# Attention scores on one core: stores that read each partition's part of a tile as one run and write it as two

## The chip, the core and the metric

The kernel runs on one core of a Trainium2 chip. The metric is the device time of one execution in microseconds (us). A core has five engines that the profile names: PE (matrix products; its weight loads are shown apart as PEld), DVE (vector), ACT (scalar), POOL and SP. SP does no arithmetic here: it waits for semaphores and issues transfers. Transfers between the chip's memory (HBM) and the core's on-chip memory (SBUF, 128 partitions) are carried by 16 DMA engines, which the trace records packet by packet.

## What is computed

Scores of attention for 8 batches of 8 heads, each 512 rows of 64 numbers:

```python
def setup_inputs():
    batch, heads, seq, dim = 8, 8, 512, 64
    ...
def reference(q, k):
    scale = 1.0 / np.sqrt(q.shape[-1])
    return (np.einsum('bhqd,bhkd->bhqk', q, k) * scale).astype(np.float32)
```

Inputs are 16.78 MB, the output (8, 8, 512, 512) in float32 is 67.11 MB. All of both must pass the DMA engines once.

## The kernel before

**Tiles.** The output is made in 16 tiles of 4 MB, numbered `g`. Tile `g` belongs to batch `2 * (g // 4) + g % 2`. In one tile a partition holds 8 consecutive rows (`i`, `RO = 8`) of one head, and it does so for two heads (`x` = 0, 1). Eight rows of 512 float32 are 16 KB, so a partition's part of a tile is two blocks of 16 KB, 32 KB in all. In SBUF these two blocks lie one after the other: `big` has, for each partition, the shape (4 buffers, 2, 8, 512), and `bigs[g % 4]` is the buffer of tile `g`. In the output array the two blocks lie 4 MB apart (4 heads further on), and the blocks of neighbouring partitions lie side by side.

**Loads.** The four 2 MB slices of keys and of queries are loaded into the same buffers `big`. The first slice of keys is loaded in two halves of 1 MB, in pieces of 4 KB, one issued by SP and one by ACT (L72). The other seven (L83) are issued by SP one after the other, with runs of 16 KB on both sides.

**Compute.** POOL casts the loaded data to bf16 (`xb`, L126). DVE transposes keys into `kT` (L194) and queries into `qz` (L199). PE multiplies (L152): for each tile 16 products, in four groups of four, each group filling half of PSUM (the accumulation memory). ACT, or DVE for six of the groups, scales a group of four and writes it to `big` (L173, L171). Semaphores named `low*`, `high*`, `pe` and `out` order these; `free0` and `free1` count when a pair of buffers has been stored and may be overwritten.

**Stores.** SP's queue runs, after the loads, a loop over the tiles. Tile 0 is stored by itself as soon as `pe` shows that its last group has been taken, tile 1 by itself when `out` shows that it is complete (both L95, 4 MB each). From then on tiles 2 and 3, 4 and 5, and so on are stored in pairs, seven times 8 MB (L98), each when `out` counts the pair as complete. A pair occupies buffers 0 and 1 or buffers 2 and 3, so there are two pairs of buffers: while one pair is being stored, compute fills the other. When a store has landed it adds to `free0` or `free1`, and PE waits for that before it begins the next pair of tiles in these buffers.

The order of the work on each queue is written out by hand; there is no scheduler. Everything that the change touches is SP's store loop, lines 85 to 102 of the kernel before: the two calls of `dma_start` at L95 and L98. Each takes the tile as 128 partitions by 2 (or 4) pieces of 4096 numbers (16 KB) and the output in the same shape, where piece `b x` of the output is block `x` of batch `b`.

Of the kernel before, what the change touches and what calls it, by code (L numbers as in the profile page):

```python
# [5 lines left out]
def kernel(  # L6
# [5 lines left out]
    nc = tc.nc  # L12
# [4 lines left out]
    UNITS = B // 2  # L17
# [33 lines left out]
    big = nc.alloc_sbuf_tensor("big", [P, UNITS, 2, RO, S], f32)[:]  # L51
    bigs = [big[:, n] for n in range(UNITS)]
# [10 lines left out]
    def xf(v):  # L63
        return bigs[v].rearrange("p x i k -> p (x i k)").rearrange("p (x s c) -> p x s c", x=2, s=2)

    def slot(v, x):
        return v % SLOTS * 2 + x
# [3 lines left out]
    for s, queue in enumerate((nc.sync, nc.scalar)):  # L71
        first_load = queue.dma_start(  # L72
            out=xf(0)[:, 0, s].rearrange("p (x c) -> p x c", x=2), in_=k_0[s]
# [7 lines left out]
    for n in range(1, 2 * UNITS):  # L81
        v, x = divmod(n, 2)
        nc.sync.dma_start(out=xf(v)[:, x].rearrange("p s c -> p (s c)"), in_=(k_r, q_r)[x][v]  # L83
                          ).then_inc(load_sems[n], 16)
    for g in range(ALL):
        if g % 2:
            nc.sync.wait_ge(sem["out"], g // 2 + 1)
        elif g == 0:
            nc.sync.wait_ge(sem["pe"], 4 * g + 6)
        else:  # L90
            continue
        dst = out_r[g // 4, g // 2 % 2]
        free = sem[f"free{g // 2 % 2}"]
        if g < 2:
            nc.sync.dma_start(out=dst[:, g % 2 * 2:g % 2 * 2 + 2],  # L95
                              in_=bigs[g].rearrange("p x i k -> p x (i k)")).then_inc(free, 16)
        else:
            nc.sync.dma_start(out=dst, in_=big[:, g % UNITS - 1:g % UNITS + 1].rearrange(  # L98
                "p n x i k -> p (n x) (i k)")).then_inc(free, 32)
        if g % 2 and g < ALL - 1:  # L100
            nc.sync.sem_inc(sem[f"free{1 - g // 2 % 2}"], 1)  # L101
    for n in range(2):
# [4 lines left out]
    for v in range(UNITS):  # L107
# [3 lines left out]
        for x in range(2):  # L111
            if v or x:
                nc.gpsimd.wait_ge(load_sems[2 * v + x], 16)
            for s in range(2):
# [3 lines left out]
                dst = xb[:, slot(v, x)]  # L118
                if x == 0:
                    src = src.rearrange("p (w e d) -> p w e d", e=2, d=D)  # L120
                    dst = dst[:, s * J // 2:(s + 1) * J // 2].rearrange("p w d e -> p w e d")
                else:
                    src = src.rearrange("p (jj e i d) -> p jj e i d", e=2, i=RO, d=D)
                    dst = dst.rearrange("p (i jj) d e -> p jj e i d", i=RO)[
                        :, s * JJ // 2:(s + 1) * JJ // 2]
# [9 lines left out]
    with pe.Fori(0, ALL // 4):  # L135
        for t in range(4):
# [10 lines left out]
            for x in range(2):  # L147
                for i in range(RO):
                    if (x, i) in waits:
                        name, count = waits[x, i]  # L150
                        pe.wait_ge(sem[name], count)
                    ins = pe.matmul(out=ps[:, i], lhsT=qz[:, 2 * t + x, i], rhs=kT[:, 2 * t + x],  # L152
                                    start=True, stop=True)
                    if i % W == W - 1:
                        ins.then_inc(sem["pe"], 1)
                    elif (x, i) in takes:
                        name, count = takes[x, i]
# [105 lines left out]
```

## Time and profile before

| What | Value |
|---|---|
| time, median of 4 runs | 200.41 us (200.35 to 200.59) |
| time of the profiled execution | 200.4 us |
| its span, first to last instruction | 199.1 us |
| busy: PE / DVE / ACT / POOL | 82.3 / 113.9 / 105.9 / 38.9 us |
| moved by DMA | 83.90 MB: 16.78 read from HBM, 67.11 written |
| mean rate over the span | 421 GB/s |
| stores issued (SP's queue) | 2 of 4096 KB, 7 of 8192 KB |
| start of the stores' issue, us | 36.15, 42.13, 58.23, 78.28, 98.02, 117.15, 136.70, 156.29, 176.10 |
| time to issue a store / a load of L83 | 0.38 to 0.44 / 0.58 to 0.62 us |

The span is what the profiler saw between the first and the last instruction; the 1.3 us between it and the execution's time lie around it. The busy times of the engines add up to more than the span because they work side by side. A transfer is issued at one time and moves its bytes later: it stands behind earlier transfers of the same queue.

### The profile page before, as it was taken

The page shows a single profiled execution, that of the slowest core. Times are in us where ns is not written, and L with a number is a line of the kernel's source. Part 1 is how long each engine was busy: PE and PEld are TensorE (multiplying, and loading weights), DVE is VectorE, ACT ScalarE, POOL GpSimd, SP SyncE. Part 2 cuts the span into 40 slices and gives each one's busy share as a digit, 9 for nine tenths or more (in the row PEclk, how much of TensorE's full clock was granted, in tenths as well). Part 3 has the DMA queues.
Part 4 walks back from the last instruction along what each step waited for, and adds up shares of the span by engine and source line. Part 5 has one row for each costly group of instructions (what it writes and reads, how often), then busy time and mean ns, then how long its engine had stood idle before and what let it go on. Part 6 is the DMA issues. An engine that isn't in the chain of part 4 may idle for free.

```text
span 199.1 us, 725 instructions
## 1 busy us (share of the span) xinstructions
PE 82.3 (41%) x252; PEld 23.9 (12%) x256; DVE 113.9 (57%) x61; ACT 105.9 (53%) x59; POOL 38.9 (20%) x20
## 2 busy tenths in 40 slices
PE   0000357647524762576266516650776077600000
PEld 0000011111101110111021102110221021100000
DVE  4238999999477039943994599369926500400000
ACT  2000049969960977197629752974397349730000
POOL 0389999699000000000000000000000000000000
PEclk9999999988975799669859985999589658975555
DMA  6999999999999999999999999999999999999997
GB/s 182 444 428 425 435 428 431 428 418 431 428 431 438 425 438 428 431 435 425 435 428 438 431 426 435 423 438 435 428 435 425 435 438 425 435 425 428 425 431 316
DMA packets 5794, 83.90 MB, mean 421 GB/s; under 512 B 288, under 2 KB 288, under 8 KB 800
## 3 DMA queue, kind: packets, MB, share of 16 engines
q1 hardware_dynamic: 5520, 82.84, 97.8%
q10 hardware_dynamic: 272, 1.05, 1.3%
q14 instruction: 2, 0.02, 0.0%
HBM read 16.78 MB, written 67.11 MB: 421 GB/s over the span
## 4 chain that ended last, share of the span: by engine, by line
DMA 41%; ACT 30%; PE 9%; DVE 4%; POOL 2%; issue 1%; SPq 0%
DMA out_dram<-big 35%; ACT big L173 30%; PE ps L152 9%; DMA big<-in_q_dram 6%; DVE qz L199 4%; POOL xb L126 2%; SPq L95 0%; SPq L101 0%
## 5 line engine op out<-in xcount | busy, mean ns | idle before, releaser
L173 ACT ACTIVATE big<-ps 128x2048 f32<-128x2048 f32 x58 | 104.6, 1884 | 68.2 <-PE ps L152 68.2
L152 PE MATMUL ps<-kT,qz 128*128 128x512 bf16 x252 | 82.3, 465 | 91.7 <-DMA out_dram<-big 35.8
L199 DVE STREAM_TRANSPOSE qz<-xb 32x1024 f32<-32x1024 f32 (+1 forms) x36 | 65.2, 1810 | 1.5 <-POOL xb L126 0.9
L152 PEld LDWEIGHTS ps<-kT,qz 128*128 128x128 bf16 x256 | 23.9, 111 | 149.7 <-ACT big L173 47.9
L126 POOL CAST xb<-big 128x2048 bf16<-128x2048 f32 x16 | 38.7, 2468 | 10.4 <-DMA big<-in_k_dram 7.7
L171 DVE TENSOR_SCALAR big<-ps 128x2048 f32<-128x2048 f32 x6 | 13.8, 2292 | 43.8 <-PE ps L152 43.8
L194 DVE STREAM_TRANSPOSE kT<-xb 64x1024 f32<-64x1024 f32 (+1 forms) x18 | 31.5, 1749 | 10.9 <-POOL xb L126 6.7
L206 DVE MEMSET qz<- 128x4096 uint32 x1 | 3.5, 3472 | 2.9 <-PEq L77 2.9
L173 ACT ACT_TABLE_LOAD x1 | 1.3, 1283 | 2.0 <-PEq L77 2.0
L247 POOL MEMSET const-float32-0.0<- 128x1 f32 x1 | 0.1, 99 | 0.2 <-issue 0.2
L247 POOL MEMSET const-bfloat16-1.0<- 128x1 bf16 x1 | 0.1, 102 | 0.0
L247 POOL MEMSET const-uint8-127<- 128x1 uint8 x1 | 0.1, 102 | 0.0
L247 POOL MEMSET const-float32-1.0<- 128x1 f32 x1 | 0.1, 99 | 0.0
## 6 DMA issues: line engine op xcount, KB each, us to landing
out_dram<-big SPq DMA_DIRECT2D x7, 8192.0 KB
big<-in_q_dram SPq DMA_DIRECT2D x4, 2048.0 KB, 24.2
out_dram<-big SPq DMA_DIRECT2D x2, 4096.0 KB
big<-in_k_dram SPq DMA_DIRECT2D x3, 2048.0 KB, 24.2
big<-in_k_dram SPq DMA_DIRECT2D x1, 1024.0 KB, 7.4
big<-in_k_dram ACTq DMA_DIRECT2D x1, 1024.0 KB, 9.7
```

The costliest lines, as they stand in the source:

```text
L126: cast = nc.gpsimd.tensor_copy(out=dst, in_=src)
L152: ins = pe.matmul(out=ps[:, i], lhsT=qz[:, 2 * t + x, i], rhs=kT[:, 2 * t + x], start=True, stop=True)
L171: freed = nc.vector.tensor_scalar_mul(out=to, in0=src, scalar1=scale)
L173: freed = nc.scalar.mul(out=to, in_=src, mul=scale)
L194: return nc.vector.transpose(out=out, in_=src)
L199: return nc.vector.transpose(out=qw[d:d + Q, b % 2 * G:(b % 2 + 1) * G, rows, h * Q:(h + 1) * Q].rearrange("d g i (m jj) -> d i jj m g", j ...
L206: nc.vector.memset(qz, 0.0).then_inc(sem["zeroed"], 1)
L247: nc = _bacc.Bacc("TRN2", target_bir_lowering=False, num_devices=1)
```

## The change

The stores are no longer issued by `dma_start`, which gives both sides of a transfer the same shape. A new helper `store` builds the copy instruction itself. It takes the tile in SBUF as 128 partitions by 1 (or 2) runs of 8192 numbers (32 KB), and the output as 128 partitions by 2 (or 4) runs of 4096 numbers (16 KB) as before. Bytes, their order, addresses, the queue, the waits before the stores and the semaphores after them are the same. Loads and all work on the other engines are as before. The instruction is also no longer marked as precomputed by the building library, as `dma_start` marked the stores of before (the loads have no such mark in either kernel).

```diff
+    def store(to, tiles):
+        run = tiles.rearrange("p n x i k -> p n (x i k)")
+        return nc.sync.add_instruction(mybir.InstDMACopy(
+            name=nc.get_next_instruction_name(), engine=mybir.EngineType.SP, mode="Copy",
+            queue="qSPDynamicHW", ins=nc.sync.lower_ap_dma(run), outs=nc.sync.lower_ap_dma(to)))
+
     for g in range(ALL):
         if g % 2:
             nc.sync.wait_ge(sem["out"], g // 2 + 1)
...
         if g < 2:
-            nc.sync.dma_start(out=dst[:, g % 2 * 2:g % 2 * 2 + 2],
-                              in_=bigs[g].rearrange("p x i k -> p x (i k)")).then_inc(free, 16)
-        else:
-            nc.sync.dma_start(out=dst, in_=big[:, g % UNITS - 1:g % UNITS + 1].rearrange(
-                "p n x i k -> p (n x) (i k)")).then_inc(free, 32)
+            store(dst[:, g * 2:g * 2 + 2], big[:, g:g + 1]).then_inc(free, 16)
+        else:
+            store(dst, big[:, g % UNITS - 1:g % UNITS + 1]).then_inc(free, 32)
         if g % 2 and g < ALL - 1:
             nc.sync.sem_inc(sem[f"free{1 - g // 2 % 2}"], 1)
```

## The prediction, made before the changed kernel ran

> **What bounds the kernel now.** I read first the row of slices and the queue table of the page, to see whether any engine or the transfers fill the span. The DMA row is a busy share in tenths over 40 slices, the GB/s row is what the 16 DMA engines moved, and the queue rows give packets, MB and share of 16 engines' span.
>
> ```profile
> DMA  6999999999999999999999999999999999999997
> GB/s 182 444 428 425 435 428 431 428 418 431 428 431 438 425 438 428 431 435 425 435 428 438 431 426 435 423 438 435 428 435 425 435 438 425 435 425 428 425 431 316
> DMA packets 5794, 83.90 MB, mean 421 GB/s; under 512 B 288, under 2 KB 288, under 8 KB 800
> q1 hardware_dynamic: 5520, 82.84, 97.8%
> ```
>
> The transfers fill the span from the second slice to the last, at a rate that hardly moves; only start-up and the last landing are left out. The busiest compute engine, DVE, is at 57%. So any time must come out of the bytes' own rate, or out of a hole that the change would tear into it.
>
> Next the chain of waits (start us, length us, what), to see whether compute ever holds the transfers up.
>
> ```profile
> 58.23 23.75 DMA out_dram<-big
> 81.98 0.05 issue
> 82.03 1.90 PE ps L152 x4
> ...
> 94.35 3.65 ACT big L173 x2
> 98.01 0.02 issue
> 98.02 22.95 DMA out_dram<-big
> ```
>
> The chain puts 30% on ACT, which misleads alone: its steps run while the store of the other pair of tiles moves. The windows view settles it, in stretches of one 8 MB store each (stretch; its length; busy time by engine; granted clock, DMA share, GB/s).
>
> ```profile
> 61.40:80.83 19.43, 10.15 (x32) 2.96 (x32) 10.12 (x6) 12.60 (x7) 0.00 (x0) 0.85 1.01 432
> 80.83:100.26 19.43, 10.49 (x31) 3.00 (x32) 13.78 (x8) 12.71 (x7) 0.00 (x0) 0.76 1.01 432
> 119.70:139.13 19.43, 9.90 (x31) 2.92 (x32) 13.98 (x8) 12.60 (x7) 0.00 (x0) 0.85 1.01 431
> ```
>
> Each stretch is as long as the last, with a DMA share just over 1: the packets' recorded times overlap a little, and no compute wait opens a hole.
>
> **What one packet costs.** 67.11 MB written in pieces of 16 KB (16,384 bytes) are 4096 packets, 256 on each of 16 engines. This checks with the q1 row: 4096 of stores, 7 loads of 2 MB in 16 KB (896), 256 of the first key load's half in 4 KB, and 16 small ones for each of 17 transfers (272) make 5520. To split a packet's time into a part for bytes and a part for being a packet, I take the transfers in two windows: 62 to 176 us, stores alone, and 4 to 7 us, where only 4 KB packets run.
>
> ```profile
> DMA packets 3086, 49.20 MB, mean 432 GB/s; under 512 B 82, under 2 KB 82, under 8 KB 82
> q1 hardware_dynamic: 3084, 49.19, 100.7%
> ```
>
> ```profile
> DMA packets 309, 1.27 MB, mean 422 GB/s; under 512 B 0, under 2 KB 0, under 8 KB 309
> q1 hardware_dynamic: 155, 0.63, 51.9%
> q10 hardware_dynamic: 154, 0.63, 51.1%
> ```
>
> In the first, 3084 less 82 small ones are 3002 data packets: 16 x 114,000 ns / 3002 = 607.6 ns from one to the next on an engine, and 100.7% of that, 611.8 ns, is what one is recorded to take. So consecutive packets overlap by 4.2 ns. In the second, 16 x 3000 / 309 = 155.3 ns from one to the next, recorded at 103.0% of it, 160.0 ns. Four small packets carry the bytes of one large one, with three more packets: (4 x 155.3 - 607.6) / 3 = 4.5 ns for being a packet (one packet more or less in the 309 moves this by 0.7), which leaves 603.1 ns for 16 KB themselves. From recorded times, as if nothing overlapped, it is (640.0 - 611.8) / 3 = 9.4 ns.
>
> The small packets are loads and the large ones stores; that the fixed part is alike in both is my assumption.
>
> **The change, part by part.** (1) *Read runs.* Each tile's 32 KB in a partition is now one read run instead of two. That removes 128 read runs on each engine, 2048 in all. If the 4.5 ns belong to the read run, or to a packet that begins and ends with it, the gain is 128 x 4.5 = 0.58 us, all of it on the path that sets the end, since the engines are never idle in the store stage. Bounds: nothing gained, if the cost goes with a written piece; at most 128 x 9.4 = 1.20 us, if the saved packet start costs all that is recorded. I take 0.58, because spacing, not recorded length, is what fills a saturated stage.
>
> (2) *Write runs.* Their number, size, order and addresses stay: 256 on each engine, 16 KB each. What is new is that one read run feeds two of them. The trace of before has no such transfer. From below it costs nothing, or repays what (1) has; from above, the overlap between the pieces is lost (256 x 4.2 = 1.08 us). Farthest out, both written pieces and the read each pay 9.4 ns one after another: 128 x (3 x 9.4 - 2 x 4.5) = 2.46 us. I take nothing: the nearest row, 603.1 ns of bytes in 607.6, says that an engine streams one run into the next with almost no seam, and a seam inside one run should be no worse than that.
>
> (3) *Issue on SP.* The store's instruction is made by hand, with different shapes on its two sides. In the SP queue's rows (start us, us, engine, line) a store of before takes 0.40 us to issue and a load, whose two sides also differ in shape, 0.58.
>
> ```profile
> 2.65 0.58 SPq L83 DMA_DIRECT2D big<-in_k_dram  x1
> 78.28 0.40 SPq L98 DMA_DIRECT2D out_dram<-big  x1
> 98.02 0.39 SPq L98 DMA_DIRECT2D out_dram<-big  x1
> ```
>
> At worst that is 0.2 us more for each of 9 stores. Its cover is the store before: the one issued at 58.23 lands at 81.98, and the next is issued at 78.28, 3.70 us earlier. The first issue of the program, at 0.73, has moved no byte by 1.8 us in the trace, so about 1.1 us are start-up; allow another 1 us (an estimate from the last stretch, where the rate has fallen to 316 GB/s) between last byte and landing, and some 1.6 us are spare. So I cost it at nothing; were the cover gone, it would be 9 x 0.2 = 1.8 us. What is late next would be PE, which waits for the landing that frees a pair of tiles. No wait is added, and on PE, DVE, ACT and POOL nothing changes.
>
> Sum, against the profiled execution's own 200.4 us (span 199.1 and 1.3 around it): 200.4 - 0.58 + 0 + 0 = 199.8. The median of the runs is 200.41, so it holds there as well.
>
> The Trainium skill, page "DMA: Bandwidth & Descriptors", section "Why small descriptors are slow (HBM only)", names a fixed cost of about 3 cycles for a packet on trn2 beside 32 bytes a cycle; at the 850 MHz that the page gives for the fabric this is 3.5 ns and an estimate of 128 x 3.5 = 0.45 us, hence 199.95. The same section speaks against this change: it calls joining descriptors "only worth it at ≤256 B desc size", by which the sum would be nothing at 16 KB, 200.4. The windows above put a price on the packet at 16 KB, so here the size of the run does not make it free, only small.
>
> **The rivals.** *No change (200.4).* The 4.5 ns go with the written piece, of which there are as many as before, or the read run is cut again at 16 KB on its way, so that the change does not do what it says. For it: a record of before counts one packet per 16 KB and cannot tell which side it belongs to. Against it: only that reads and writes have the same number there, so nothing excludes it. The gain also falls into this case when a saved packet is worth under 0.40 / 128 = 3.1 ns; my 4.5 is not far above.
>
> *Slower (201.5).* At the seam inside the 32 KB run the second write cannot begin in the shadow of the first one's end, as separate packets do now: the 4.2 ns of overlap go at every piece, 1.08 us and 200.4 + 1.08 = 201.5, up to 202.9 by the far bound. It decides from 3.1 ns lost net in each 32 KB. For it: the overlap in the trace is one between packets, and the new packets are half as many; the stage has no idle time to hide any of it. Against it: bytes stream at 603.1 of 607.6 ns, which leaves little to lose. The late issue of (3) belongs to the slower side too, but needs 1.6 us to start.
>
> **How the numbers follow.** About 0.2%, 0.40 us, is what a measurement of this kernel can tell from no change. Forecast of a saved read run, 199.8, own range 199.2 to 200.0: 0.53. No change, 200.0 to 200.8: 0.23. Slower, at 201.5 for the most part: 0.24, of which 0.02 is the late issue. The likeliest gives the time, 199.8. The range starts at the largest gain, 200.4 - 1.20 = 199.2, takes in no change and reaches to the slower rival's 201.5; about 0.1 lies above, where the far bound is or the seam costs what no row shows, and 0.03 below.
>
> **What would show it.** Right: the stretch of one 8 MB store shrinks from 19.43 us to 19.43 - 16 x 0.0045 = 19.36 us, with the store window at about 433 to 434 GB/s, and the loads' part unchanged. If records follow read runs, q1 falls from 5520 to 3472 packets with a mean near 1215 ns; if they follow writes, the count stays and tells nothing. No change: stretches stay at 19.43. Slower: they grow to 19.5 or more with the DMA share still near 1 (a seam), or with slices under 9 between stores (late issue). I am wrong if the stretches stay while the total moves, or if a store's rate changes by over 1% either way, which no price above allows.

## The result and the profile after

The changed kernel takes 200.13 us (median of 40 runs, 199.96 to 200.30) against 200.41 us (60 runs, 200.29 to 200.62): 0.28 us less, a ratio of 0.9986 with a 95% interval of 0.9981 to 0.9990. The sign is the one forecast and the time lies in the range, but the gain is half of the 0.58 us predicted. It is under the 0.2% that the prediction took as the least that can be told from no change; the interval, a gain of 0.20 to 0.38 us, does tell it. The profiled execution took 200.05 us, with a span of 198.7.

The same rows of the page as before, now of the changed kernel:

```profile
GB/s 198 435 439 435 432 422 429 429 455 442 422 422 422 422 422 442 455 449 435 429 429 422 422 424 422 450 442 442 442 429 422 422 429 422 422 455 455 442 429 231
DMA packets 3746, 83.90 MB, mean 422 GB/s; under 512 B 288, under 2 KB 288, under 8 KB 800
q1 hardware_dynamic: 3472, 82.84, 97.2%
```

The trace counts read runs: q1 falls from 5520 packets to 3472, by exactly the 2048 reads removed. The change does what it says. (The rate of a slice now swings between 422 and 455 because a packet is entered whole where it starts, and a slice holds only four or so of them per engine.)

The stretches of one 8 MB store each, in the windows view of the changed kernel (stretch; length; busy time by engine; granted clock, DMA share, GB/s). Every engine closes a store with a packet of 4 bytes; the bounds, here and before, are where the first of the 16 engines does so.

```profile
61.28:80.65 19.37, 9.81 (x32) 2.89 (x32) 10.72 (x6) 12.60 (x7) 0.00 (x0) 0.85 1.00 433
80.65:100.02 19.37, 10.21 (x31) 3.01 (x32) 14.05 (x8) 12.60 (x7) 0.00 (x0) 0.76 1.00 433
119.39:138.76 19.37, 9.62 (x31) 2.89 (x32) 14.21 (x8) 12.60 (x7) 0.00 (x0) 0.85 1.01 433
177.51:196.88 19.37, 0.00 (x0) 0.00 (x0) 0.00 (x0) 0.00 (x0) 0.00 (x0) 0.50 1.00 433
```

19.37 us in place of 19.43, where 19.36 was predicted. So the DMA engine that leads saves nearly all that was forecast, and yet the end moves by half of it. The end is set by the engine that comes last. Its lag shows when the closing packets are counted in the transfers of two windows, the row's "under 512 B". Before:

```profile
DMA packets 14, 0.03 MB, mean 66 GB/s; under 512 B 12, under 2 KB 12, under 8 KB 12
...
DMA packets 4, 0.00 MB, mean 0 GB/s; under 512 B 4, under 2 KB 4, under 8 KB 4
```

That is 197.7 to 198.2 us, and 198.2 to 198.7: 12 engines close the last store in the first half microsecond, 4 in the next. After, in 196.8 to 197.5 and 197.5 to 198.3:

```profile
DMA packets 15, 0.03 MB, mean 47 GB/s; under 512 B 14, under 2 KB 14, under 8 KB 14
...
DMA packets 2, 0.00 MB, mean 0 GB/s; under 512 B 2, under 2 KB 2, under 8 KB 2
```

Fourteen engines are done by 197.5, earlier than the first one before (197.71), and two stragglers set the end, the last at 198.23 where the last before was 198.60. From the first engine to the last it was 0.89 us before and is 1.34 us after. (These are two single executions, 200.40 and 200.05 us; by the medians the gain is 0.28.) That is the place where expected gain went missing; the experiments ask what a read run is worth, and what the stragglers owe their lag to.

### The profile page after: what moved, and what is told of

The parts are those of the page before. It is cut to its first block, busy times and chain, and to the rows that moved or that the text cites. A ratio compares the mean times of both kernels' runs of the same rounds, so it can differ in the third digit from the quotient of the medians.

```text
span 198.7 us, 725 instructions
## 1 busy us (share of the span) xinstructions
PE 81.2 (41%) x252; PEld 23.7 (12%) x256; DVE 113.9 (57%) x61; ACT 105.7 (53%) x59; POOL 38.9 (20%) x20
## 3 DMA queue, kind: packets, MB, share of 16 engines
q1 hardware_dynamic: 3472, 82.84, 97.2%
## 4 chain that ended last, share of the span: by engine, by line
DMA 41%; ACT 33%; PE 6%; DVE 4%; POOL 2%; issue 0%; SPq 0%
DMA out_dram<-big 35%; ACT big L179 33%; PE ps L158 6%; DMA big<-in_q_dram 6%; DVE qz L205 4%; POOL xb L132 2%; SPq L89 0%; SPq L107 0%
## 5 line engine op out<-in xcount | busy, mean ns | idle before, releaser
L158 PE MATMUL ps<-kT,qz 128*128 128x512 bf16 x252 | 81.2, 459 | 92.3 <-DMA out_dram<-big 35.4
L212 DVE MEMSET qz<- 128x4096 uint32 x1 | 3.5, 3472 | 2.9 <-PEq L77 2.9
```

The lines of the kernel that those rows point to most:

```text
L212: nc.vector.memset(qz, 0.0).then_inc(sem["zeroed"], 1)
```

## The experiments

Three groups of runs: the cost of each side's runs, transfers without compute, and the same with a hole ahead of the stores.

### What belongs to the instruction, and what to the run

**equal16_byhand.** The changed kernel's helper, with 16 KB runs on the read side.

```diff
-        run = tiles.rearrange("p n x i k -> p n (x i k)")
+        run = tiles.rearrange("p n x i k -> p (n x) (i k)")
```

> The helper of the changed kernel, but with 16 KB runs on both sides, as the kernel before has them: only the way in which the instruction is made, and with it its issue on SP, differs from before. Theory (the gain is the saved read run or packet start): no gain is left, 200.41 us within 0.1, with 5520 packets on q1 in records of about 611 ns, and issues of about 0.61 us, as in the changed kernel, hidden behind the store before. Rival (the gain comes from the hand-made instruction): 200.13.

Measured 200.42 us against 200.40 of the kernel before beside it, ratio 1.0001 (0.9992 to 1.0010). On the page and in SP's queue (start us, us, engine, line):

```profile
q1 hardware_dynamic: 5520, 82.84, 97.7%
```

```profile
77.98 0.64 SPq L89 DMA_DIRECT2D out_dram<-big  x1
```

The issue is as long as in the changed kernel (0.64 us at 77.86 there, 0.40 before), and costs nothing that can be measured. The gain comes from the joined read runs and not from the way in which the instruction is made.

**flat_r32_w16, flat_r32_w32, flat_r32_w8.** The output's rows land in other places here, so that a partition's bytes are one stretch in HBM, and read and written runs can be chosen one by one (32 KB reads with 16, 32 or 8 KB writes). This is the edit for 16 KB writes; `e` in the first pair of lines is the read run in numbers of 4 bytes, in the second the written piece:

```diff
+    flat = out.rearrange("b h q k -> (b h q k)")
...
-        run = tiles.rearrange("p n x i k -> p n (x i k)")
+        run = tiles.rearrange("p n x i k -> p (n x i k)").rearrange("p (c e) -> p c e", e=8192)
...
-            store(dst, big[:, g % UNITS - 1:g % UNITS + 1]).then_inc(free, 32)
+            store(flat[(g - 1) * 2 ** 20:(g + 1) * 2 ** 20].rearrange("(p c e) -> p c e", p=P, e=4096), big[:, g % UNITS - 1:g % UNITS + 1]).then_inc(free, 32)
```

> The changed kernel with other addresses in the output: each partition's part of a tile or pair goes to one contiguous stretch of the output (rows land in other places), in the same 16 KB writes, fed by the same 32 KB reads. It is the base for the runs with other sizes. Both theories: 200.13 us if the distance between the two written blocks costs nothing. If far-apart blocks cost something, it is faster than that.

> As the base with contiguous output, but written in 32 KB runs as well: read and written runs are equal in number again, at half the number of before. Theory (a read run or packet start costs, a further written piece is free): the same as the base, within 0.1 us. Rival (a written piece costs as much as the read run, and a joined read saves only half of what a joined pair would): 128 x 3.5 ns = 0.45 us faster than the base, 199.7.

> As the base with contiguous output and 32 KB reads, but written in 8 KB pieces: 256 more written pieces on each engine. Theory (written pieces inside one read run are free): the same as the base, within 0.1 us. Rival (a written piece costs about 3.5 ns): 0.9 us slower than the base, 201.0.

Measured in this order, each against 200.40: 200.05 us (ratio 0.9982, 0.9973 to 0.9991), 200.11 (0.9985, 0.9976 to 0.9994) and 200.31 (0.9993, 0.9984 to 1.0002). Joining the written runs as well brings no time, against the rival that a written piece costs as much as a read run. But 8 KB pieces cost something, against the expectation that they are free. The stretches tell it apart, here two with 32 KB writes and then one with 8 KB:

```profile
61.23:80.59 19.36, 10.10 (x32) 2.97 (x32) 10.10 (x6) 12.60 (x7) 0.00 (x0) 0.85 1.00 433
80.59:99.95 19.36, 10.55 (x32) 3.02 (x32) 13.79 (x8) 12.71 (x7) 0.00 (x0) 0.76 1.01 435
```

```profile
61.45:80.90 19.45, 10.26 (x32) 3.02 (x32) 10.50 (x7) 12.60 (x7) 0.00 (x0) 0.76 1.00 431
```

**flat_r16_w8, flat_r8_w8.** The other way: two 8 KB pieces written for each 16 KB read, and 8 KB on both sides, by the sizes `e` of the same two lines.

> Full kernel, contiguous output, 16 KB reads as before, each written as two 8 KB pieces. Theory (the read run costs, a second written piece within it about 1 ns): 256 x 1.2 = 0.3 us slower than the kernel before at most, 200.4 to 200.7. Rival (a written piece costs like a read run): 201.6, like the run with 8 KB on both sides.

> Full kernel, contiguous output, 8 KB runs on both sides: 256 more read runs and 256 more written pieces on each engine than with 16 KB on both (512 each). Theory (about 4.6 ns for each packet that begins with a read run): 256 x 4.6 = 1.2 us slower than the kernel before, 201.6, with records near 309 ns. If the end follows an engine that is late for other reasons, less than that.

Measured 200.56 us against 200.40 (1.0012, 1.0003 to 1.0020), as expected: written pieces are not priced like read runs. (Its stretch 61.46 to 80.93 takes 19.47 us, which is 0.04 / 32 = 1.3 ns for each added seam between two written pieces.) With 8 KB on both sides 202.85 us (1.0122, 1.0108 to 1.0137), twice the expected loss. Its stretches show two regimes:

```profile
61.63:81.21 19.58, 10.54 (x32) 3.02 (x32) 10.44 (x6) 12.71 (x7) 0.00 (x0) 0.76 1.01 428
...
120.65:140.68 20.03, 9.88 (x32) 2.91 (x32) 13.91 (x8) 12.60 (x7) 0.00 (x0) 0.84 1.01 419
```

At first a store takes 0.15 us more than before for 32 more read runs on each engine, (19.58 - 19.43) / 32 = 4.7 ns each, as predicted (4.6). From about 100 us on it takes 20.0. Something else sets in. By size, (20.03 - 19.58) / 64 = 7.0 ns for each read run, it is what the runs with a hole show further below; but in the trace from 130 to 132 us the starts of the packets do not gather as they do there, so its cause stays open.

From these stretches, taken over four stores (77.73 us before, 77.48 in the changed kernel, 77.43 with 32 KB writes): a saved read run is worth (77.73 - 77.43) / 64 = 4.7 ns, and the seam between two written pieces costs (77.48 - 77.43) / 64 = 0.8 ns, which leaves 3.9 ns for each join in the changed kernel, 0.50 us over its 128. (The bounds are read to 0.01 us, which moves each of these prices by some 0.2 ns.)

### Transfers alone, with and without a hole

All work on PE, DVE, ACT and POOL is left out in the next four runs; the loaded data is stored in place of scores, in the same nine stores.

**bare_r16_w16, bare_r32_w16.** The stores begin when all loads have landed.

```diff
+    for n in range(1, 2 * UNITS):
+        nc.sync.wait_ge(load_sems[n], 16)
...
+        if n >= 2:
+            nc.sync.wait_ge(landed[n - 2], 16)
```

> Transfers alone: all loads, then, once these have landed, the nine stores, each issued when the one two before it has landed; no work on PE, DVE, ACT and POOL, so that the loaded data is stored instead of scores. Reads and writes of a store in 16 KB runs. It is the base of the next run. The bytes are those of before; waiting for the loads opens one hole of some 2 us, so about 202 us. If one DMA engine is late because of the compute beside it, the 16 engines end within 0.6 us of each other here; if it is late by itself, they end as far apart as in the kernel before, 0.9 us or more.

> The same transfers alone, with the changed kernel's 32 KB reads. Theory (every engine saves 3.5 to 4 ns at each of 128 joined reads, and in the full kernel one engine, disturbed while compute runs, keeps part of it from the end): 0.45 to 0.5 us faster than the run with 16 KB reads. Rival (that engine is slow by itself, or the saving is only the 0.28 us that the full kernel shows): 0.28 us faster or less.

Measured 203.19 us (1.0137, 1.0122 to 1.0152) and 201.81 (1.0072, 1.0059 to 1.0085): 1.38 us apart, far from both expectations. All 16 engines end within 0.23 and 0.22 us, as expected if the spread comes from compute. But every store is slower. The windows of the run with 16 KB reads (only POOL, clock, share and rate are left in the row), and then of that with 32 KB:

```profile
63.78:83.44 19.66, 0.00 (x0) 1.00 1.01 427
```

```profile
63.79:83.26 19.47, 0.00 (x0) 1.00 1.00 431
```

That is 0.23 us over 19.43 for 32 read runs, and 0.10 over the changed kernel's 19.37 for 16: 6 to 7 ns more for each read run, of 16 KB or of 32. My new theory was that the hole, after which all 16 engines start at once, leaves them in step, and that starting a run costs more when all engines start one together.

**nohole_bare_r16, nohole_bare_r32.** The same transfers, but each store waits for the loads of its own buffers alone, so the queue never runs empty.

```diff
-    for n in range(1, 2 * UNITS):
-        nc.sync.wait_ge(load_sems[n], 16)
...
+        for m in ((1,), (2, 3), (4, 5, 6, 7))[n] if n < 3 else ():
+            nc.sync.wait_ge(load_sems[m], 16)
```

> Transfers alone again, 16 KB reads, but the first stores are issued behind the loads of their own buffers, so that the queue never runs empty and the engines come into the stores as far apart as in the full kernel. Theory (the 203.19 us of the run with a hole come from the 16 engines starting the stores in step, and a packet start costs more in step): an 8 MB store takes 19.43 us as in the full kernel in place of 19.65, and the whole 200.2 us or less. Rival (the absence of compute, or the queue's order, makes packets slower): 19.65 us per store remain, and only the hole of some 2 us is gone, 201.2.

> The same without the hole, with 32 KB reads. Theory (out of step a joined read saves 3.5 to 4 ns, and no engine is disturbed by compute): 0.45 to 0.5 us faster than the same run with 16 KB reads, more if that one falls into step later on. Rival (the 1.38 us between the two runs with a hole is the true saving without compute): 1.3 us or more.

Measured 199.89 us (0.9977 of the kernel before, 0.9968 to 0.9987) and 199.39 (0.9951, 0.9937 to 0.9965): 0.50 us apart, as the theory had it, and as 128 x 3.9 ns give; the two intervals leave some 0.2 and 0.3 us to either side of the times. The step can be seen. Here are 4 us of transfers, 90 to 94, in 40 slices of 0.1 us, in which a packet is entered where it starts; first with the hole, then without, both with 16 KB reads:

```profile
GB/s 0 0 1147 1311 164 0 0 0 1147 1311 164 0 0 0 1147 1311 164 0 0 0 983 1475 164 0 0 0 819 983 819 0 0 0 492 1311 819 0 0 0 492 1147
```

```profile
GB/s 328 492 164 655 164 819 328 492 164 655 164 655 492 492 164 492 328 655 328 492 328 328 492 655 328 328 492 328 492 655 328 328 492 164 655 655 328 328 492 164
```

With the hole the 16 engines start their packets within some 0.2 us of each other, every 0.6 us; without it the starts are spread over the whole 0.6 us. Late in the run without a hole (16 KB reads) they fall into step by themselves, at 189 to 193 us:

```profile
GB/s 0 1147 819 492 164 0 0 1147 819 492 164 0 0 492 1311 655 164 0 0 328 1475 492 328 0 0 0 1802 492 328 0 0 0 1638 655 328 0 0 0 1475 655
```

and the store there takes longer, where that of the run with 32 KB reads does not:

```profile
61.39:80.82 19.43, 0.00 (x0) 1.00 1.01 432
...
158.55:178.15 19.60, 0.00 (x0) 1.00 1.00 428
```

```profile
61.43:80.79 19.36, 0.00 (x0) 1.00 1.00 433
...
158.25:177.62 19.37, 0.00 (x0) 1.00 1.00 433
```

The kernel before has a late loss of the same size: 19.56 us for the stretch 158.56 to 178.12, and 19.59 for the last. From 189 to 193 us, however, its starts gather in two groups for each 0.6 us, not in one, so that it is the same thing is not shown.

**hole_r16_w16, hole_r32_w16.** The full kernels again (16 KB reads by the helper, and the changed kernel), with SP waiting for all loads ahead of the first store.

```diff
+    for n in range(1, 2 * UNITS):
+        nc.sync.wait_ge(load_sems[n], 16)
     for g in range(ALL):
```

> The full kernel with 16 KB reads and writes, correct output, but SP waits until all loads have landed before the first store: a hole of some 1 to 2 us in which all engines run empty and after which they start in step. Theory (in step, a packet start costs about 7 ns more): stores of 19.65 us at least at the beginning, so slower than before by the hole and up to 1.8 us more, 202.5 to 204. If step does not matter: the hole alone, 201.5 to 202.5, with stores of 19.43.

> The changed kernel with the same wait for all loads. Theory: in step a joined read saves about 10 ns in place of 3.5 to 4, so this is 0.8 to 1.3 us faster than the same kernel with 16 KB reads. If step does not matter: 0.28 us faster, as without the hole.

Measured 203.62 us (1.0164, 1.0150 to 1.0179) and 202.18 (1.0091, 1.0077 to 1.0106): 1.44 us apart, a little over the expected 0.8 to 1.3. The hole is about 2 us long, and the stores after it take what they took without compute:

```profile
63.64:83.29 19.65, 10.55 (x32) 3.00 (x32) 10.62 (x7) 12.71 (x7) 0.00 (x0) 0.76 1.01 427
```

```profile
63.50:82.99 19.49, 9.91 (x32) 2.91 (x32) 10.73 (x7) 12.60 (x7) 0.00 (x0) 0.85 1.00 430
```

So the dearer start does not come from compute being absent. Nor is it some other mark that the hole leaves on all transfers: in both runs one engine is held up at about 119 us and from then on closes its stores last, nearly 1 us out of step with the others. With 16 KB reads it closes at 123.51, 142.94 and 162.38 us, 19.43 us a store, while the engine that leads takes 19.64 and 19.66; with 32 KB reads it takes 19.37 us for each of four stores, while the leader takes 19.42 to 19.52. The engine out of step pays the price of the runs without a hole.

### What compute costs the last engine

In the run without compute and hole, with 32 KB reads, the distance from first to last engine is 0.61 us at the end of the loads and 0.61 at every store up to the end. The transfers of 196.9 to 197.65 us hold all 16 closing packets:

```profile
DMA packets 16, 0.00 MB, mean 0 GB/s; under 512 B 16, under 2 KB 16, under 8 KB 16
```

In the changed kernel the distance is 0.47 us when the store that ends at 80.65 closes, then 0.60, 0.87, 0.98, 1.15 and 1.34 at those that follow, and it stays at 1.34 in the last store, beside which no compute runs.

The records do not name the engine, but its packets can be followed, since each begins some 4 ns before the one ahead of it ends. Followed so, it is one engine that falls behind, store after store. It closes its stores at these times (us):

| Kernel | Closing packets of the engine that ends last |
|---|---|
| before | 61.61, 81.19, 100.79, 120.38, 139.98, 159.56, 179.16, 198.60 |
| changed | 61.52, 81.06, 100.63, 120.18, 139.74, 159.28, 178.85, 198.23 |

Beside compute it takes 19.58 to 19.60 us for a store before, where the leader's undisturbed stretch is 19.43, and 19.54 to 19.57 after, where it is 19.37: some 0.16 and some 0.19 us lost at each store. In the last store, without compute, it takes 19.44 and 19.38. So beside compute a store of this engine gains only 0.03 to 0.04 us by the change, and over all seven it gains 136.99 - 136.71 = 0.28 us, which is the size of the whole kernel's gain, in place of the 0.44 that 112 joins at 3.9 ns give. `equal16_byhand` again has such an engine, from 61.58 to 198.57 us (136.99), and `flat_r32_w16` too, from 61.58 to 198.30 (136.72); the runs without compute have none. What in the compute slows this one engine is not shown.

The other straggler of the changed kernel, which closes at 197.76, has another mark. The transfers of 116 to 130 us, in the kernel before and then in the changed one, hold this:

```profile
q14 instruction: 2, 0.02, 0.3%
```

```profile
q1 hardware_dynamic: 197, 5.93, 98.5%
q14 instruction: 2, 0.02, 0.3%
```

Two fetches of 8 KB of program, 0.31 us each, run on these engines; the runs without compute have none. In the changed kernel the engines that are held up at that time close by 197.76, so the fetches do not set the end; and the kernel before has the same two.

In times: compute costs 200.41 - 199.89 = 0.52 us with 16 KB reads, and 200.13 - 199.39 = 0.74 us with 32 KB. The difference, 0.22 us, is what is missing from 0.50 to 0.28. The intervals of the times are too wide to show it by themselves; the traces account for 0.44 - 0.28 = 0.16 of it over the last seven stores.

## Why the prediction was right, and where it was off

*What bounds the kernel.* Right. The stretches follow the price of a packet to 0.01 us, and the issue that grew by 0.2 us changed nothing. One reading was too smooth: the three stretches shown are alike, but the last two of the seven take 19.56 and 19.59 us.

*Part (1), 128 read runs at 4.5 ns.* Right: 4.7 ns by the stretches with 32 KB and with 8 KB on both sides. Taking the price from the spacing, and not from the recorded lengths (9.4 ns), was the right choice, and loads of 4 KB gave a price that holds for stores of 16 KB. That it came so close is luck in part, since one packet more or less in the 309 would have moved it by 0.7. The Trainium skill ("DMA: Bandwidth & Descriptors", "Why small descriptors are slow (HBM only)") has about 3 cycles a packet, by its 850 MHz an estimate of 3.5 ns, which is nearer to the net 3.9 of a join. Its sentence that concatenating descriptors is "only worth it at ≤256 B desc size" gave the prediction no gain at 16 KB; here a join saves 3.9 ns of 1210 (19.37 us / 16), small but not nothing, and over 10 with the engines in step.

*Part (2), the seam at nothing.* Mis-sized, slightly: 0.8 ns, 128 x 0.8 = 0.10 us. The reason given, that a seam inside a run is no worse than one between runs, held. With 8 KB writes the seams add up: three in each 32 KB run, (19.45 - 19.36) / 48 = 1.9 ns each, and a store of 19.45 us has nothing left of the gain.

*Part (3), the issue.* Right: 0.57 to 0.67 us in place of 0.38 to 0.44, behind the store before.

*The sum.* This is the step that failed: "all of it on the path that sets the end, since the engines are never idle in the store stage". The engines are never idle, but the end is that of the last of 16, and beside compute one of them is slower than the rest. What the leading engine saves, 0.06 us a store, comes through whole where no compute runs (0.50 us), and only to 0.28 where it does: the last engine saves 0.03 to 0.04 a store beside compute, 0.28 us over the seven of 8 MB. Of the predicted 0.58 us, then, 0.08 went to prices (the seam, less a slightly dearer run) and 0.22 by the medians to the last engine. The page's rows, means over 16 engines, could not show that; the closing packets of each store could have.

*The rivals.* By size the result lies where the no-change case was drawn, within 0.2%, but by its mechanism it is the forecast's. No change because the cost sits on the written piece: refuted by the time with 32 KB writes (200.11 beside 200.05). Read runs cut again: refuted by the packet count. Slower by the lost overlap: refuted by the stretches.

*What stays open.* Which compute work delays the one slow engine, why only that one, and why it loses more at a store with 32 KB reads (0.19 us) than with 16 KB (0.16). Nor is it shown why the engines fall into step late in a run without a hole, and what the late losses of the kernel before and of the run with 8 KB on both sides are.

No version tried beats the changed kernel: the contiguous layout, which puts the rows in other places and so is no replacement, has with 32 KB reads the same time within the intervals (0.9982, 0.9973 to 0.9991, beside 0.9986, 0.9981 to 0.9990).

## What to carry to other kernels

Where transfers fill the span, price a packet by its spacing in two windows of different packet size; that price held to 0.2 ns here, closer than its own uncertainty of 0.7. Then ask which of the DMA engines ends last, because a saving on all of them reaches the end only as far as the last one keeps it. And avoid a moment in which all engines run empty in the middle of a stream: here it cost not only the 2 us of the hole, but about 7 ns at every later read run of the engines in step.

## What the runs showed of the hardware

- A read run has a price, a written piece inside it a smaller one: 4.7 ns for a read run, 0.8 ns for a 16 KB seam, 1.3 to 1.9 ns for an 8 KB one.
- Without compute and with 32 KB reads the 16 engines kept their distance from each other, 0.61 us, over 150 us. A hole brings them into step (within 0.23 us), where each read run costs some 7 ns more: 1.38 and 1.44 us between 16 and 32 KB reads in place of 0.28 to 0.50. An engine that is thrown out of step pays the lower price again (19.43 and 19.37 us a store).
- Beside compute one of the 16 engines lost 0.16 us (16 KB reads) or 0.19 us (32 KB) at each 8 MB store, and it set the end of both kernels in the executions profiled.
- Issuing a store whose two sides have different shapes, or one made by hand with equal shapes, took 0.6 us in place of 0.4.
